# Layer with two head groups: x requested one column set ahead, its scaling and transposes paced anew, second token tile four steps behind, bonus matmuls three steps later

## The chip, the cores and the metric

The kernel runs on one core of a Trainium2 chip. The metric is device time in microseconds (us) of one execution, the median of several. Engines are named as in the profile: PE is TensorE (matmuls and transposes), ACT is ScalarE, DVE is VectorE, POOL is GpSimd, SP is SyncE, which here issues nearly all DMAs, in order, in one queue.

## The reference, cut to what matters

One layer on x of 4096 tokens by 1024 (float32): a normalised input is projected by one matrix to 4224 columns, which feed two groups of heads.

```python
xn = rms_norm(h, norm_g[l], RMS_EPS)
proj = xn @ w_in[l]
...
rwkv_in = token_shift(proj[..., off_b:off_b + SHIFT_WIDTH], shift_mu[l])
r, k_b, v_b, wd, ad = jnp.split(rwkv_in, b_idx, axis=-1)
...
y = rwkv7_recurrence(r_h, hd_b(decay), k_h, v_h, kk, hd_b(a))
...
bonus = jnp.sum(r_h * k_h * r_k[l].astype(f32), axis=-1, keepdims=True) * v_h
o_b = (y + bonus.reshape(bsz, seq, W_RWKV)).astype(x.dtype) * jax.nn.silu(g_b)
...
mix = jnp.concatenate([o_a, o_b], axis=-1)
h = h + mix @ w_out[l]
return rms_norm(h, final_g, RMS_EPS)
```

Group A is softmax attention (left out above), group B the recurrence.

## The kernel before, in words

Three phases follow one another: phase 1 (projection, and beside it the recurrence), phase 2 (attention), phase 3 (output projection). The change touches phase 1 alone.

**Projection.** The tokens are cut into eight blocks of 512. For a block the scaled x lies transposed in SBUF as `xh` (rounded) and `xl` (the remainder), eight slices of 128 by 512 each; there is one such pair, overwritten block after block, in two halves of 256 tokens. A block has an r set (columns of group B) and an a set (group A). The sets are worked off in the order r0 a0 r1 a1 r2 a2 r3 r4 r5 r6 r7 a7 a6 a5 a4 a3. Each set is a row of jobs. Token jobs (`tm_part`, kinds VB, GB, V, GA; one stands first and one last in every set) make four token tiles of 128 by 512; feature jobs (`fm_groups`) make one or two feature tiles. A step is one call of `mm3`, three matmuls (L248, L249, L250): L248 and L249 read `xh`, L250 reads `xl`. A token job has two parts of 16 steps; in each part the second tile runs two steps behind the first. Steps of a token job are counted 0 to 31 below, and those of the job after it go on from 32. Weight tiles `w` come through a ring of eight: `release` frees one and issues the load of the one eight further on (L233). Results stand in three PSUM buffers `pjt`/`pjf`; those of GB and GA are read by ACT (L310) and then DVE (L311), after which the buffer is free.

**New tokens.** Where the block changes (11 times), the last job of a set brings the first half of the next block: `x_load` (two DMAs into the two buffers `xv`, L153), `x_norm` (two squares on ACT into PSUM buffers `jk`, L162; an addition on DVE; two POOL operations; a scaling on ACT, L166), then `x_trans`: four groups of four PE transposes into a PSUM buffer `pt` (L176), each followed by two copies on ACT (`xh`, L179) and two remainders on DVE (`xl`, L180). In the second part of that job the four groups stand after steps 17, 20, 23 and 26, and `x_load` of the second half at step 27. The first token job of the next set carries the second half: scaling after step 4 (36), transposes after steps 6, 8, 10 and 12 (38, 40, 42, 44).

**Recurrence.** Four generators share PE with the projection. After each step `tick` lets every one that isn't waiting run on; a generator that gave a negative number runs only at every fourth tick. `p1_unit` prepares 256 tokens (16 units, two halves each); its last part is the bonus: POOL multiplies (L506), eight small PE matmuls take the product (`pbn`, L524), ACT copies it out. Key a8 of the table W is the number of ticks from the stage before to these matmuls. `p2_unit` inverts small triangles on DVE (31 times L578 and L579), `c_stream` walks the 64-token chunks (PE L687, DVE L690, PE L695 and L702, DVE L712, PE L716 and L721, DVE L725 and L728), `o_stream` finishes group B. They use three PSUM buffers `pg` in turn, `jk` and `pt` too. PE's order is as the program writes it; on the other engines a scheduler sets the order when the program is built.

Of the kernel before, what the change touches and what calls it, by code (L numbers as in the profile page):

```python
# [25 lines left out]
W = dict(  # L26
    G=4,    xn=2, xl=1024, sw=1024, np=2, le=3, l0=8, gb=5, pj=3, sb=4, wb=8, tb1=7, wm=0,
    xw=2048, cw=512, pl=1, pelat=330, tb=3, pb=3, lag2=2.0, ms=40, a0=2, a1=2, a2=2, a3=2,
    a4=2, a5=2, a6=2, a7=2, a8=2, a9=2, b0=2, b1=2, b2=2, b3=2, b4=2, b5=2,
    b6=2, b7=2, b8=1, b9=1, c0=10, c1=8, c2=2, c3=2, c4=1, c5=1, c6=2, c7=3,  # L30
    c8=2, o0=2, o1=4, o2=2, o3=4, o4=2, o5=2, o6=1, held=5, el=1, pz=18, ld=14,
    ba=2,  df=[2, 2, 2, 2],
# [76 lines left out]
def _phase1(ctx, tc, nc, e):  # L109
# [38 lines left out]
    def x_load(b, t):  # L148
        xs = []
        for s in range(2):  # L150
            r0 = b * BT + t * 256 + s * 128
            xv = xp.tile([128, D], F32, tag="xv", name="xv", bufs=2)
            nc.sync.dma_start(xv, x[r0:r0 + 128, :])  # L153
            xs.append(xv)
        xraw[b, t] = xs
# [105 lines left out]
                yield  # L261
            evacs[p](po)

    def tm_part(n0, s0, evac, last, side_x):
        po = {}
        order = []
        for n in range(KD + 2):
            if n < KD:
                order.append((s0, n))
            if n >= 2:  # L270
                order.append((s0 + 1, n - 2))
        for s, k in order:
            if k == 0:
                po[s] = ps_j.tile([128, BT], F32, tag="pj", name="pjt")
            w = wt[n0 + k]
            sl = slice(128 * s, 128 * s + 128)
            mm3(po[s], xh[:, k, sl], xl[:, k, sl], w[:, 0].rearrange("p a c -> p (a c)"), w[:, 1].rearrange("p a c -> p (a c)"), k)
            if k == KD - 1:
                evac(s)(po[s])
            if last and s == s0 + 1:  # L280
                release(n0 + k)
            next(side_x, None)
            yield
# [33 lines left out]
    def paced(g, steps):  # L317
        for n in range(64):
            if n in steps:
                next(g, None)  # L320
            yield

    def x_half1(b):
        x_norm(b, 1)
        yield
        yield from x_trans(b, 1)
        if b == 0:
            xfree[0] = True
            raw_next()
# [6 lines left out]
    def x_norm0(b):  # L336
        x_norm(b, 0)
        yield

    def tile_job(i, kind, parts, evs, nxt):  # L340
        n0 = first_tile[i]
        if kind == "f":
            assert not bg
            yield from fm_groups(n0, parts, [ev(0) for ev in evs])
            return
        half1 = bg.pop(1, None)
        assert half1 is None or nxt is None
        if nxt is not None:
            x_load(nxt, 0)
        if half1 is not None:  # L350
            side = paced(x_half1(half1), (4, 6, 8, 10, 12, 13))
        else:
            side = paced(x_norm0(nxt) if nxt is not None else iter(()), (10,))
        yield from tm_part(n0, 0, evs[0], False, side)
        for _ in side:
            pass
        side = paced(x_half0(nxt) if nxt is not None else iter(()), (1, 4, 7, 10, 11))
        yield from tm_part(n0, 2, evs[0], True, side)
        for _ in side:
            pass  # L360
        if nxt is not None:
            bg[1] = nxt
# [34 lines left out]
    def main():  # L397
        x_norm(0, 0)
        yield from x_trans(0, 0)
        x_load(0, 1)  # L400
        bg[1] = 0
        for _ in range(RING):
            prep()
        for i, (k, parts, evs, nxt, rdone) in enumerate(jobs):
            yield from tile_job(i, k, parts, evs, nxt)
            if rdone:
                done_r[0] += 1
# [1044 lines left out]
```

## Time and profile before

| | us |
|---|---|
| median of 3 runs | 3769.85 (3767.56 to 3772.0) |
| the profiled execution | 3761.58 |
| its span, first to last instruction | 3759.9 |
| busy in the span: PE, DVE, ACT, POOL | 3609.4, 2632.4, 1922.4, 761.2 |

The profile names a group of instructions by source line, engine, operation and tiles (written<-read). An instruction's idle time is that of its engine just before it, with what ended it. The granted clock is TensorE's, as a share of full speed (2.4 GHz). Phase 1 ends at 2135 us of the span, phase 2 at about 3380.

### The profile page before, as it was taken

The page shows a single profiled execution, that of the slowest core. Times are in us where ns is not written, and L with a number is a line of the kernel's source. Part 1 is how long each engine was busy: PE and PEld are TensorE (multiplying, and loading weights), DVE is VectorE, ACT ScalarE, POOL GpSimd, SP SyncE. Part 2 cuts the span into 40 slices and gives each one's busy share as a digit, 9 for nine tenths or more (in the row PEclk, how much of TensorE's full clock was granted, in tenths as well). Part 3 has the DMA queues.
Part 4 walks back from the last instruction along what each step waited for, and adds up shares of the span by engine and source line. Part 5 has one row for each costly group of instructions (what it writes and reads, how often), then busy time and mean ns, then how long its engine had stood idle before and what let it go on. Part 6 is the DMA issues. An engine that isn't in the chain of part 4 may idle for free.

```text
span 3759.9 us, 69957 instructions
## 1 busy us (share of the span) xinstructions
PE 3609.4 (96%) x26370; PEld 3050.9 (81%) x26370; DVE 2632.4 (70%) x5882; ACT 1922.4 (51%) x4042; POOL 761.2 (20%) x1156
## 2 busy tenths in 40 slices
PE   7999999999999999998999999999999999989999
PEld 5777777777777778777777789999999999978887
DVE  3566666667767787757777588898898898863333
ACT  4452352444445443444444377787787787761111
POOL 0112211211212222212221032222222222211000
PEclk9999999999999999999999999999999999999999
DMA  7976665666555565665675651141141131033332
GB/s 231 354 267 204 209 212 198 222 204 225 192 192 190 191 226 174 215 209 196 221 239 200 204 122 48 41 113 37 49 104 49 38 82 40 21 134 121 134 134 74
DMA packets 346092, 593.60 MB, mean 158 GB/s; under 512 B 55193, under 2 KB 210329, under 8 KB 345754
## 3 DMA queue, kind: packets, MB, share of 16 engines
q1 hardware_dynamic: 344602, 587.62, 48.4%
q8 instruction: 208, 3.41, 0.4%
q10 hardware_dynamic: 1152, 1.51, 0.1%
q14 instruction: 130, 1.06, 0.1%
HBM read 434.85 MB, written 154.14 MB: 157 GB/s over the span
## 4 chain that ended last, share of the span: by engine, by line
PE 75%; DVE 13%; DMA 4%; ACT 3%; issue 2%; SPq 2%; POOL 1%; DVEq 0%; POOLq 0%; ACTq 0%
PE po L1222 12%; PE ps L1127 6%; PE ps L1126 6%; PE tp L1197 6%; PE pjf L248 5%; PE pjf L250 4%; PE pjf L249 4%; PE pjt L248 4%; PE pjt L250 4%; PE pjt L249 4%; PE po L1372 3%; PE po L1371 3%; PE po L1370 3%; DVE DG L578 2%; DVE TL L579 2%
## 5 line engine op out<-in xcount | busy, mean ns | idle before, releaser
L1159 ACT ACTIVATE ring<-ring,nm 128x2048 f32<-128x2048 f32 (+14 forms) x472 | 589.0, 1253 | 31.3 <-DVE nm L1151 30.2
L1141 DVE CUSTOM_DVE_ANT_0 ring<-ps,zcol 128x1024 f32<-128x1024 f32 (+6 forms) x464 | 485.2, 1058 | 109.2 <-PE ps L1127 103.1
L1222 PE MATMUL po<-v,pt 128*128 128x128 f32 x4224 | 539.5, 276 | 10.0 <-ACT pt L1210 5.4
L1222 PEld LDWEIGHTS po<-v,pt 128*128 128x128 f32 x4224 | 517.9, 192 | 28.5 <-ACT pt L1210 7.3
L1126 PE MATMUL ps<-k,ta 128*128 128x512 f32 (+3 forms) x1152 | 483.1, 420 | 7.3 <-DMA ta<-q_d 4.9
L248 PE MATMUL pjt<-w,xh 128*128 128x512 f32 x1024 | 436.2, 426 | 29.1 <-DMA w<-ws_d 13.4
L248 PE MATMUL pjf<-xh,w 128*128 128x512 f32 x1088 | 451.1, 415 | 6.0 <-ACT w L236 4.5
L1127 PE MATMUL ps<-k,tb 128*128 128x512 f32 (+3 forms) x1152 | 432.0, 379 | 0.0
L250 PE MATMUL pjf<-xh,w 128*128 128x512 f32 x1088 | 431.0, 396 | 0.5 <-DVE w L237 0.5
L249 PE MATMUL pjf<-xl,w 128*128 128x512 f32 x1088 | 429.9, 395 | 0.0
L249 PE MATMUL pjt<-w,xh 128*128 128x512 f32 x1024 | 410.5, 401 | 0.9 <-DVE w L237 0.9
L250 PE MATMUL pjt<-w,xl 128*128 128x512 f32 x1024 | 410.0, 401 | 0.1
L1182 DVE SCALAR_TENSOR_TENSOR ring<-ring,rho 128x512 f32<-128x512 f32 (+3 forms) x600 | 407.1, 702 | 1.6
L1210 ACT COPY pt<-tp 128x512 f32<-128x512 f32 (+3 forms) x576 | 303.1, 550 | 194.0 <-PE tp L1197 188.7
L1197 PE MATMUL tp<-ident,ring 128*128 128x128 f32 x2112 | 313.6, 274 | 3.7 <-DVE ring L1182 3.7
L1197 PEld LDWEIGHTS tp<-ident,ring 128*128 128x128 f32 x2112 | 254.6, 142 | 40.6 <-issue 3.7
L248 PEld LDWEIGHTS pjt<-w,xh 128*128 128x128 f32 x1024 | 199.0, 194 | 80.9 <-DMA w<-ws_d 20.3
L248 PEld LDWEIGHTS pjf<-xh,w 128*128 128x128 f32 x1088 | 207.3, 191 | 57.4 <-ACT w L236 6.5
L250 PEld LDWEIGHTS pjf<-xh,w 128*128 128x128 f32 x1088 | 207.0, 190 | 49.2 <-DVE w L237 2.7
L1126 PEld LDWEIGHTS ps<-k,ta 128*128 128x128 f32 x1152 | 219.2, 190 | 32.8 <-issue 5.0
L1127 PEld LDWEIGHTS ps<-k,tb 128*128 128x128 f32 x1152 | 220.1, 191 | 23.4
L249 PEld LDWEIGHTS pjf<-xl,w 128*128 128x128 f32 x1088 | 208.0, 191 | 38.1
(205 smaller groups left out, 6421.4 us busy)
## 6 DMA issues: line engine op xcount, KB each, us to landing
w<-ws_d SPq DMA_DIRECT2D x448, 512.0 KB, 5.3
ws_d<-w SPq DMA_DIRECT2D x64, 512.0 KB, 5.3
xv<-in_x_dram SPq DMA_DIRECT2D x48, 512.0 KB, 5.4
ta<-q_d SPq DMA_DIRECT2D x128, 128.0 KB, 2.9
tb<-q_d SPq DMA_DIRECT2D x128, 128.0 KB, 3.0
k<-k_d SPq DMA_DIRECT2D x32, 512.0 KB, 7.1
mi<-mix_d SPq DMA_DIRECT2D x32, 512.0 KB, 3.3
xi<-in_x_dram SPq DMA_DIRECT2D x32, 512.0 KB, 4.2
```

Source lines behind the costliest of these rows:

```text
L248: nc.tensor.matmul(po, ah, bh, start=(k == 0), stop=False)
L249: nc.tensor.matmul(po, ah, bl, start=False, stop=False)
L250: nc.tensor.matmul(po, al, bh, start=False, stop=(k == KD - 1))
L1126: nc.tensor.matmul(ps[:, c:c + w], rr(ta[:, m, qs]), rr(k[:, m, c:c + w]), start=True, stop=False)
L1127: nc.tensor.matmul(ps[:, c:c + w], rr(tb[:, m, qs]), rr(k[:, m, c:c + w]), start=False, stop=True)
L1141: nc.vector.tensor_tensor_reduce(rg(m, ro, x), st["ps", b, m][:, c - 1024 * b:c - 1024 * b + x], msk, 0.125, -3.0e38, ALU.add, ALU.max, ac ...
L1159: nc.scalar.activation(rg(m, ro, x), rg(m, ro, x), AF.Exp, bias=st["nm"][:, m:m + 1], accum_out=st["lp"][:, m, j:j + 1])
L1182: nc.vector.scalar_tensor_tensor(rg(0, ro, x), in0=rg(1, ro, x), scalar=st["rho"], in1=rg(0, ro, x), op0=ALU.mult, op1=ALU.add)
L1197: nc.tensor.transpose(tp[:, j], rg(0, c, 128), ident)
L1210: nc.scalar.copy(pt[:, :n], st.pop(("tp", g))[:, :n])
L1222: nc.tensor.matmul(st["po"], pt[:, j], vt[h, kb // 8][:, kb % 8], start=(kb == 0), stop=(kb == i))
L1370: nc.tensor.matmul(po, mh[:, k], wh[k][:, fs], start=(k == 0), stop=False)
```

## The change

The first half of x is asked for one job earlier (before the job ahead of the last one), unless the last job's weights come fresh from the input, which is so at the first of the 11 changes of block; its scaling then stands at step 3 in place of 10, and its transposes after steps 16, 19, 21 and 24, with `x_load` of the second half at step 25. For that second half (not in block 0) the scaling moves to step 5 of the next token job (37) and the transposes to steps 12, 14, 17 and 20 (44, 46, 49, 52): two groups now stand inside its second part. In the second part of every token job the second tile runs four steps behind the first, so weight tiles 0 to 4 of such a job are released at steps 21, 23, 25, 27, 28 in place of 19, 21, 23, 25, 27. a8 goes from 2 to 5.

```diff
-    a4=2, a5=2, a6=2, a7=2, a8=2, a9=2, b0=2, b1=2, b2=2, b3=2, b4=2, b5=2,
+    a4=2, a5=2, a6=2, a7=2, a8=5, a9=2, b0=2, b1=2, b2=2, b3=2, b4=2, b5=2,
...
-    def tm_part(n0, s0, evac, last, side_x):
+    def tm_part(n0, s0, evac, last, side_x, lag):
         po = {}
         order = []
-        for n in range(KD + 2):
+        for n in range(KD + lag):
             if n < KD:
                 order.append((s0, n))
-            if n >= 2:
-                order.append((s0 + 1, n - 2))
+            if n >= lag:
+                order.append((s0 + 1, n - lag))
...
+        if half1 is not None:
+            side = paced(x_half1(half1), (5, 12, 14, 17, 20, 21) if half1 else (4, 6, 8, 10, 12, 13))
+        elif nxt is not None:
+            if (nxt, 0) not in xraw:
+                x_load(nxt, 0)
+                side = paced(x_norm0(nxt), (10,))
+            else:
+                side = paced(x_norm0(nxt), (3,))
+        else:
+            side = iter(())
+        yield from tm_part(n0, 0, evs[0], False, side, 2)
         if nxt is not None:
-            x_load(nxt, 0)
-        if half1 is not None:
-            side = paced(x_half1(half1), (4, 6, 8, 10, 12, 13))
-        else:
-            side = paced(x_norm0(nxt) if nxt is not None else iter(()), (10,))
-        yield from tm_part(n0, 0, evs[0], False, side)
-        for _ in side:
-            pass
-        side = paced(x_half0(nxt) if nxt is not None else iter(()), (1, 4, 7, 10, 11))
-        yield from tm_part(n0, 2, evs[0], True, side)
+            for _ in side:
+                pass
+            side = paced(x_half0(nxt), (0, 3, 5, 8, 9))
+        yield from tm_part(n0, 2, evs[0], True, side, 4)
...
         for i, (k, parts, evs, nxt, rdone) in enumerate(jobs):
+            if i + 1 < len(jobs) and jobs[i + 1][3] is not None and not tiles[min(first_tile[i + 1], len(tiles) - 1)][3]:
+                x_load(jobs[i + 1][3], 0)
             yield from tile_job(i, k, parts, evs, nxt)
```

The request for x on SP's queue, at the change from block 1 to block 2. First the order before: the two `xv` loads that end the excerpt's middle are the first half of block 2.

```order
L314 DMA ga_d<-st 128x512
L314 DMA vb_d<-st 128x512
L153 DMA xv<-in_x_dram 128x1024 x2
L314 DMA vb_d<-st 128x512
L233 DMA w<-ws_d 128x1024 x8
```

And in the changed kernel:

```order
L314 DMA ga_d<-st 128x512
L314 DMA vb_d<-st 128x512 x2
L153 DMA xv<-in_x_dram 128x1024 x2
L233 DMA w<-ws_d 128x1024 x3
L314 DMA vb_d<-st 128x512
```

In both these loads stand in the first job of the set, right behind the second half of block 1, some 100 rows ahead of the job that scales them; one store of `vb_d` has moved ahead of them.

PE around the third group of transposes of a second half, at the change from block 4 to block 5; `xv_10069` and `xv_10071` (`xv_10020` and `xv_10022` in the changed kernel) are its tokens, and the numbers of `w` tell the weight tile, so the slice. Before:

```order
L176 MATMUL pt_10229<-ident_71,xv_10071 128x128
L248 MATMUL pjt_10150<-w_10067,xh_123 128x512
L249 MATMUL pjt_10150<-w_10067,xh_123 128x512
L250 MATMUL pjt_10150<-w_10067,xl_124 128x512
L248 MATMUL pjt_10132<-w_10125,xh_123 128x512
L249 MATMUL pjt_10132<-w_10125,xh_123 128x512
L250 MATMUL pjt_10132<-w_10125,xl_124 128x512
L176 MATMUL pt_10251<-ident_71,xv_10069 128x128
```

And now:

```order
L176 MATMUL pt_10245<-ident_71,xv_10022 128x128
L248 MATMUL pjt_10238<-w_10018,xh_123 128x512
L249 MATMUL pjt_10238<-w_10018,xh_123 128x512
L250 MATMUL pjt_10238<-w_10018,xl_124 128x512
L248 MATMUL pjt_10238<-w_10040,xh_123 128x512
L249 MATMUL pjt_10238<-w_10040,xh_123 128x512
L250 MATMUL pjt_10238<-w_10040,xl_124 128x512
L248 MATMUL pjt_10238<-w_10051,xh_123 128x512
L249 MATMUL pjt_10238<-w_10051,xh_123 128x512
L250 MATMUL pjt_10238<-w_10051,xl_124 128x512
L176 MATMUL pt_10273<-ident_71,xv_10020 128x128
```

Before, the steps behind the group work on the first half's tokens. Now they are those of tile `pjt_10238`, which is made of the second half: its third step (`w_10051`, slice 4) reads what this group has just transposed, two steps behind it.

The end of phase 1 on DVE, from the last but one `svu<-svu,WC` to the first instruction of phase 2. Before:

```order
L728 TENSOR_TENSOR svu<-svu,WC 64x256 x2
L690 COPY xs<-pc 128x256
L712 TENSOR_TENSOR svu<-pc,RN 64x256 x2
L725 TENSOR_TENSOR svu<-pc,svu 64x256 x2
L728 TENSOR_TENSOR svu<-svu,WC 64x256 x2
L757 TENSOR_REDUCE nm<-yv 128x8
L311 SCALAR_TENSOR_TENSOR st<-st,pjt 128x512
L758 SCALAR_TENSOR_TENSOR yv<-nm,yv 128x512
L1141 ISA ring,mx<-ps,mz 128x128
```

And now (each line of the source stands seven further down):

```order
L735 TENSOR_TENSOR svu<-svu,WC 64x256 x2
L311 SCALAR_TENSOR_TENSOR st<-st,pjt 128x512
L697 COPY xs<-pc 128x256
L719 TENSOR_TENSOR svu<-pc,RN 64x256
L311 SCALAR_TENSOR_TENSOR st<-st,pjt 128x512
L719 TENSOR_TENSOR svu<-pc,RN 64x256
L732 TENSOR_TENSOR svu<-pc,svu 64x256 x2
L735 TENSOR_TENSOR svu<-svu,WC 64x256 x2
L764 TENSOR_REDUCE nm<-yv 128x8
L1148 ISA ring,mx<-ps,mz 128x128
```

The last chunk of the recurrence now stands behind both last readings of `pjt`; on PE its last two groups, which stood 12 and 4 steps ahead of the projection's end, stand behind its last matmul. All along phase 1 the triangles and the chunks stand 8 steps later against the projection than before, the bonus matmuls of a unit's two halves 12 and 16 (4 and 8, then 12 and 16, up to block 3).

## Rows read from the trace of the kernel before

**Rows 1.** Windows: busy us (and count) per engine, granted clock, DMA share, GB/s.

```profile
140.00:2135.00 1995.00, 1906.75 (x15504) 1542.46 (x15504) 1369.15 (x3037) 843.08 (x1894) 418.31 (x415) 0.98 0.64 212
```

**Rows 2.** Waits of PE, 140 to 2135 us: total us, times, longest.

```profile
PE pt L176 <- ACT xv L166: 19.8, 15, 4.1
PE pjt L248 <- DMA w<-ws_d: 13.4, 12, 2.9
PE pbn L524 <- POOL rr L506: 13.3, 3, 5.2
PE pt L176 <- DVE xl L180: 11.9, 5, 4.5
PE pjt L248 <- DVE st L311: 11.7, 7, 4.0
```

**Rows 3.** Windows around two stalls.

```profile
1044.00:1058.00 14.00, 10.30 (x48) 8.42 (x48) 9.41 (x16) 9.98 (x22) 4.49 (x5) 0.88 0.31 85
1282.00:1298.00 16.00, 13.03 (x96) 10.46 (x96) 10.56 (x18) 9.62 (x23) 3.50 (x3) 0.68 0.68 219
```

**Rows 4.** Timeline of PE (start, us, then the instruction) behind another stall.

```profile
1176.40 0.63 PE L249 MATMUL pjt<-w,xh 128*128 128x512 f32 x1
1176.83 0.63 PE L250 MATMUL pjt<-w,xl 128*128 128x512 f32 x1
...
1181.02 0.40 PE L249 MATMUL pjt<-w,xh 128*128 128x512 f32 x1
1181.25 0.40 PE L250 MATMUL pjt<-w,xl 128*128 128x512 f32 x1
```

**Rows 5.** Timeline, a second half: its loads on SP, its first transposes on PE.

```profile
1032.73 1.05 SPq L153 DMA_DIRECT2D xv<-in_x_dram  x2
...
1046.98 0.33 PE L176 MATMUL pt<-ident,xv 128*128 128x128 f32 x1 [4.13 <-ACT xv L166]
```

**Rows 6.** Timeline, the next first half: its loads on SP, its first square on ACT.

```profile
1205.82 1.06 SPq L153 DMA_DIRECT2D xv<-in_x_dram  x2
...
1304.31 0.60 ACT L162 ACTIVATE jk<-xv 128x512 f32<-128x512 f32 x1
```

**Rows 7.** Timeline of ACT and PE in the last job of set r5.

```profile
1158.42 0.60 ACT L162 ACTIVATE jk<-xv 128x512 f32<-128x512 f32 x1 [6.48 <-DVE RN L479]
...
1170.14 0.50 PE L248 MATMUL pjt<-w,xh 128*128 128x512 f32 x1 [3.73 <-DVE st L311]
```

**Rows 8.** Timeline of POOL, DVE and PE at a bonus.

```profile
1282.72 1.80 POOL L506 TENSOR_TENSOR rr<-rr,f 128x512 f32<-128x512 f32 x1 [12.77 <-DVE WC L509]
...
1282.72 2.35 DVE L513 TENSOR_TENSOR BKF<-f,lw 64x512 f32<-64x512 f32 x2
...
1284.58 1.87 PE L524 MATMUL pbn<-rks,rr 128*128 128x2 f32 x8 [4.75 <-POOL rr L506]
```

**Rows 9.** Timeline, transposes and the first remainder behind them: a loaded and a quiet case.

```profile
258.59 0.60 PE L176 MATMUL pt<-ident,xv 128*128 128x128 f32 x4
...
263.70 0.88 DVE L180 SCALAR_TENSOR_TENSOR xl<-pt,g_t,xh 128x256 fp32r<-128x256 f32 x2
...
910.39 0.60 PE L176 MATMUL pt<-ident,xv 128*128 128x128 f32 x4
...
911.53 0.48 DVE L180 SCALAR_TENSOR_TENSOR xl<-pt,g_t,xh 128x256 fp32r<-128x256 f32 x1 [1.01 <-ACT xh L179]
```

**Rows 10.** Timeline, the end of phase 1 on DVE, PE and SP.

```profile
2127.88 0.86 DVE L712 TENSOR_TENSOR svu<-pc,RN 64x256 f32<-64x256 f32 x2 [3.13 <-PE pc L695]
...
2131.02 0.69 PE L716 MATMUL pc<-svu,bkt 128*64 128x64 f32 x16
...
2132.66 0.87 DVE L728 TENSOR_TENSOR svu<-svu,WC 64x256 f32<-64x256 f32 x2
...
2133.68 0.38 SPq L1025 DMA_DIRECT2D v<-v_d  x1
...
2140.38 0.73 PE L1126 MATMUL ps<-k,ta 128*128 128x512 f32 x1 [4.87 <-DMA ta<-q_d]
```

## The prediction

> **What bounds the kernel now.** I read first the page's sum: PE is busy 3609.4 of 3759.9 us, so TensorE is the bound and other engines matter only where it waits for them. The change touches phase 1 alone, so I next took that stretch after the start-up [rows 1]: PE busy 1906.75 of 1995 us, hence 88 us idle, at a mean granted clock of 0.98. Third came the list of PE's waits there [rows 2]. Five rows bear on the edits: new tokens not yet scaled (19.8), weights (13.4), the bonus product (13.3), copies that still hold a `pt` buffer (11.9), and L311 holding a `pjt` buffer (11.7). Together that is 70 us; no other wait is aimed at.
>
> Last I looked at what an idle stretch costs afterwards. Around a 4.13 us stall the clock is 0.88 over 14 us, and around a 4.75 us stall 0.68 over 16 us [rows 3]. Behind another stall matmuls follow at a pitch of 0.43 us, and a little later at 0.23 [rows 4]: PE ran at the 1.2 GHz level and then at 2.4 again, having idled before the fall. At the low level, 0.20 of each 0.43 us is lost (0.465). The mean of 0.98 over 1995 us means 4% of the stretch, about 80 us, at the low level, which loses 37 us. I spread these over the 88 us idle: every us of idle costs some 0.42 us more, so I multiply idle time by **1.42**. This is an average: some short gaps cost nothing, and the stall at 1284 cost about 16 x 0.32 x 2 x 0.465 = 4.8 us besides its own 4.75 [rows 3, 8].
>
> **The change part by part.** The sum is made against the profiled execution, 3761.58 us; the median is 8.3 us above it, so I add that at the end. A change under 0.2% (7.5 us) can hardly be told from none.
>
> *Early request of the first half: nothing.* The order shows these loads standing a set ahead already, and so does the trace: issued at 1205.82, first read at 1304.31 [rows 6], 98 us later. If that cover were gone, a load needs some 14 us from issue to first transpose, as in rows 5, and step 0 to step 17 of the old job would just have covered it.
>
> *Earlier scaling of the first half: nothing by itself.* ACT's squares get seven more steps. In set r5 they waited 6.48 us for a shared buffer with ACT's queue behind them, and PE then stalled 3.73 us for L311 [rows 7]; such an event is counted under L311 below.
>
> *Pacing of the second half: -27.7.* From its loads at 1032.73 to its first transposes at 1046.98 are 14.25 us, of which PE waited 4.13 [rows 5]. One step takes about 1.0 us: phase 1 has 32 token tiles x 8.25 column jobs x 8 slices = 2112 steps in 2135 us. Before, the loads stood at step 27 and the first transposes at step 38, 11 us for a need of 14. Now they stand at 25 and 44, 19 us. The cover holds with 5 us to spare, and the row of 19.8 us [rows 2] should go but for about 0.3: -19.5 x 1.42 = -27.7.
>
> *What that pacing makes tight: +14.* The third group makes slices 4 and 5; the first tile of the second part reads slice 4 two steps behind it (the third step of that tile in the order), and the fourth group's slice 6 as closely. Two steps are about 2 us; in the clear they are worth 2 x 0.69 + 0.46 = 1.84 us, three matmuls a step at 0.23. Between them must lie the ACT copies and the DVE remainders. In a quiet case the remainder starts 1.0 us after its transposes end and ends 0.5 later (910.39 + 0.60, 911.53 + 0.48); in a loaded one the pair ends at 264.58 (263.70 + 0.88), 5.4 us after the transposes (258.59 + 0.60) [rows 9]. The quiet one fits, the loaded one is 3.5 us late, and a second late group adds about 1.5. There are eleven changes of block. I take two as loaded, 2 x 5 us x 1.42 = +14, nearer the quiet row because DVE works 1369 of 1995 us [rows 1] and ACT and DVE mostly had the groups done in time before. Ends: 0, and +78 if all eleven are loaded.
>
> *Second tile four steps behind: -11.4.* A token job's third and fourth tiles need a `pjt` buffer each, and L311 must have left it. The fourth now asks about 2 us later. Of 11.7 us in 7 waits, the longest 4.0 [rows 2] and the other 3.73 [rows 7] keep about 1.9 each; the small ones, 4 us together, go: -8 x 1.42. Ends: 0 (the delay only moves ACT's queue) and -16.6 (all).
>
> *The same lag for the weights: +6.* Tiles 0 to 4 are released one or two steps later in each of 32 token jobs; the next job's loads leave later and its slack falls from 11 steps to 9. SP's queue is in order, so each such load also holds back the stores and x loads behind it. PE waited 13.4 us in 12 such places [rows 2]; I take 4 us more, at 1.42. Ends: 0, and +18 if twelve places lose 1 us or more (two steps of 0.69 us bare is the most one can lose: 12 x 1.38 = 16.6, and one new place).
>
> *Bonus matmuls three ticks later: -16.* PE waited 13.3 us in three places [rows 2]; at 1284.58 it waited 4.75 for L506, which POOL could start only at 1282.72 and which took 1.80 [rows 8]. The matmuls stand about four steps later against their own unit, so waits of 4.75, 5.2 and 3.4 leave about 2 us: -11.3 x 1.42. Ends: -18.9, and 0 if the delay is eaten (first rival). Rows 8 show POOL's L506 and DVE's L513 starting in the same instant, 1282.72, and both running on. The Trainium skill (SBUF — State Buffer, "Who interferes with whom") has it otherwise: VectorE with two SBUF inputs and GpSimd share ports under a lock held for a whole instruction, and the issue order says who is blocked. By that rule L506 would wait out each L513, and this term would be near 0 and the sum near -19. This trace shows no such exclusion at that place.
>
> *Buffers `pt`: -3.5.* Of 11.9 us [rows 2] the second half's groups, now two and three steps apart, lose some 2.5; the first half's last groups are as far apart as before or closer. Ends: -17 (all go), +11 (the closer groups of all first halves wait 0.7 us more).
>
> *The end of phase 1: +4.* The recurrence stands 8 steps later, so its last two PE groups come behind the last projection matmul (2135). After that: DVE's two L712 (0.86) with an L311 between them now, about 1.7 us in all with the links; then from PE's L716 to the end of L728 2.5 us (2131.02 to 2133.53); SP's load of `v` follows L728 (2133.68), `ta` is queued behind it, and PE restarts at 2140.38, 6.85 us after L728 [rows 10]. So 11 us instead of 5.4 from the last matmul to the restart, less the 2 us of PE work moved out of the projection and its own links: +3.5 to +5. No factor, since there is one such place.
>
> *What the scheduler redraws elsewhere:* 0, ends -10 and +10; the recurrence meets other steps of the projection than before, and no row tells which.
>
> Sum: -27.7 + 14 - 11.4 + 6 - 16 - 3.5 + 4 = **-34.6**, so 3727 for the profiled execution and **3735** for the median.
>
> **The rivals.** *The bonus wait comes back (18%).* The triangles and chunks move 8 steps and the bonus more, so L506 may meet the same DVE load at another place. For it: POOL waited 12.77 us for DVE at 1282.72 [rows 8], more than the four steps gained. Against it: only three of 32 halves waited at all. Then the term of -16 is lost: 3751. The Trainium skill's lock, above, would give the same by another way, and rows 8 speak against it.
>
> *Slower: the wait moves from the transposes to the matmuls behind them (12%).* Without the +14 the sum is -48.6. Eleven second halves eat it up at 4.4 us each; at the loaded row's 5 us idle each, 7.1 with the clock, they cost 78, and the time is 3769.85 - 48.6 + 78 = 3799. For it: two steps of cover against a chain through two engines and two queues, which the old pacing did not ask for, having all groups done before the second part began. Against it: the quiet row needs only 1.5 us.
>
> *Everything fits (8%).* No late remainder, no weights lost, all `pt` and bonus waits gone: -34.6 - 14 - 6 - 13.4 - 3 = -71, so 3699.
>
> *The changes only swap waits (7%).* The pacing does what the early request would have done, and that request moves nothing [rows 6]; if ACT and DVE are late by as much in the new places as x was in the old, 3770.
>
> **How the numbers follow.** My forecast has 55%, the rivals 18, 12, 8 and 7. Predicted is the forecast's 3735. Its own range, from the ends of the tight pacing, the weights and the redrawn waits, is 3710 to 3760. The whole range takes in the bonus rival and the swapped waits above, and the nearer half of the large gain below: 3703 to 3770, leaving out the slower case and half of the best one. Faster by over 0.2%: the forecast nearly whole (52), most of the bonus rival (14) and the large gain (8), 74%. Within 0.2%: the swap and the edges of the first two, 13%. Slower: its rival and a little of the swap, 13%.
>
> **What would show it.** Right: after 140 us PE's wait of `pt` for `xv` is nearly gone, that of `pbn` is under 4 us in all, that of L311 under 5, the mean clock of the stretch is 0.99, and the gap at the end of phase 1 has grown to 8 or 9 us. A new row, `pjt` waiting for `xl` or `xh`, should hold about 10 us; at 50 the slower rival is true. The weights' row should grow by some 4. If `xv` waits remain, the load is later than its issue suggests and the first term falls; if idle time falls by 30 us but the clock stays at 0.98, the factor of 1.42 is wrong.

## The result, and the profile after

The changed kernel takes 3803.11 us (four runs, 3796.49 to 3803.45) against 3768.70 for the kernel before: a ratio of 1.0086, interval 1.0068 to 1.0103. It is slower by 34 us in these medians, and by 32 in the ratio, which is used below; 35 us less were forecast. Line numbers from 410 on stand seven higher in its profile.

Phase 1 now ends at 2171.9 us instead of 2135.0. Its busy time, columns as in [rows 1]:

```profile
140.00:2172.00 2032.00, 1916.16 (x15513) 1547.56 (x15511) 1369.35 (x3037) 840.98 (x1897) 419.21 (x415) 0.97 0.62 209
```

PE was idle 115.8 us in place of 88. PE's waits there, as in [rows 2]:

```profile
PE pjt L248 <- DMA w<-ws_d: 30.4, 28, 3.6
PE pjt L248 <- DVE st L311: 11.0, 3, 5.5
PE pa L465 <- DVE xl L180: 9.5, 4, 3.5
PE pjt L250 <- DVE xl L180: 8.9, 8, 2.0
PE pc L723 <- DVE svu L719: 8.4, 6, 3.1
PE pt L176 <- DVE xl L180: 7.3, 3, 4.1
PE ptt L620 <- ACT Zs L606: 5.8, 3, 3.5
PE pjt L248 <- DVE sl L301: 5.4, 1, 5.4
PE pjt L248 <- DVE carry L292: 4.3, 2, 2.3
...
PE pjt L248 <- ACT xh L179: 3.1, 2, 2.2
```

The aimed waits did go: `xv`, 19.8 us before, is down to 2.5, `pbn` from 13.3 to nothing. But weights have doubled, L311 has not moved, and seven rows are new or larger. To place the loss, phase 1 is cut in both kernels at the same step (924, four steps before set r3 ends). First the kernel before, then the changed one:

```profile
140.00:895.00 755.00, 726.72 (x5492) 588.00 (x5492) 500.17 (x1108) 311.64 (x695) 145.18 (x145) 0.98 0.66 224
895.00:2135.00 1240.00, 1180.03 (x10014) 954.46 (x10013) 868.99 (x1930) 531.44 (x1199) 273.13 (x270) 0.97 0.63 205
```

```profile
140.00:927.00 787.00, 736.90 (x5499) 592.75 (x5498) 494.47 (x1107) 307.70 (x691) 145.15 (x145) 0.98 0.64 216
927.00:2172.00 1245.00, 1179.25 (x10015) 954.81 (x10013) 874.88 (x1931) 533.28 (x1206) 274.06 (x270) 0.97 0.61 205
```

32 of the 37 us are lost in the first part, 22 of them as idle time (755 - 726.7 = 28.3 before, 787 - 736.9 = 50.1 now). There the sets alternate between r and a, up to step 792.

The end of phase 1, timeline of PE and SP, answers to [rows 10]:

```profile
2167.47 0.39 PE L250 MATMUL pjt<-w,xl 128*128 128x512 f32 x1
...
2170.05 0.69 PE L723 MATMUL pc<-svu,bkt 128*64 128x64 f32 x16 [1.28 <-DVE svu L719]
...
2172.70 0.38 SPq L1032 DMA_DIRECT2D v<-v_d  x1
...
2178.45 0.76 PE L1133 MATMUL ps<-k,ta 128*128 128x512 f32 x1 [5.95 <-DMA ta<-q_d]
```

From the end of the last projection matmul (2167.86) to the restart are 10.6 us.

### The profile page after: what moved, and what is told of

It reads as the page before. It is cut to its first block, busy times and chain, and to the rows that moved or that the text cites. A ratio compares the mean times of both kernels' runs of the same rounds, so it can differ in the third digit from the quotient of the medians.

```text
span 3801.1 us, 69959 instructions
## 1 busy us (share of the span) xinstructions
PE 3618.4 (95%) x26370; PEld 3055.8 (80%) x26370; DVE 2632.0 (69%) x5882; ACT 1919.1 (50%) x4042; POOL 763.0 (20%) x1156
## 3 DMA queue, kind: packets, MB, share of 16 engines
q10 hardware_dynamic: 1152, 1.51, 0.1%
## 4 chain that ended last, share of the span: by engine, by line
PE 70%; DVE 13%; DMA 4%; ACT 3%; issue 2%; POOL 1%; SPq 0%; DVEq 0%; POOLq 0%; ACTq 0%
PE po L1229 12%; PE ps L1134 6%; PE ps L1133 6%; PE tp L1204 6%; PE pjf L248 4%; PE pjf L250 4%; PE pjf L249 4%; PE pjt L248 4%; PE pjt L250 3%; PE pjt L249 3%; PE po L1379 3%; PE po L1378 3%; PE po L1377 3%; DMA w<-ws_d 2%; DVE TL L586 2%
## 5 line engine op out<-in xcount | busy, mean ns | idle before, releaser
L248 PE MATMUL pjt<-w,xh 128*128 128x512 f32 x1024 | 441.0, 431 | 61.1 <-DMA w<-ws_d 30.4
L250 PE MATMUL pjf<-xh,w 128*128 128x512 f32 x1088 | 430.6, 396 | 0.6 <-DVE w L237 0.6
L250 PE MATMUL pjt<-w,xl 128*128 128x512 f32 x1024 | 415.2, 406 | 9.0 <-DVE xl L180 8.9
L249 PE MATMUL pjt<-w,xh 128*128 128x512 f32 x1024 | 415.6, 406 | 1.1 <-DVE w L237 1.1
L250 PEld LDWEIGHTS pjt<-w,xl 128*128 128x128 f32 x1024 | 200.4, 196 | 60.5 <-DVE xl L180 15.1
L250 PEld LDWEIGHTS pjf<-xh,w 128*128 128x128 f32 x1088 | 207.0, 190 | 49.1 <-DVE w L237 2.7
```

The costliest lines, as they stand in the source:

```text
L248: nc.tensor.matmul(po, ah, bh, start=(k == 0), stop=False)
L249: nc.tensor.matmul(po, ah, bl, start=False, stop=False)
L250: nc.tensor.matmul(po, al, bh, start=False, stop=(k == KD - 1))
```

## The experiments

Times below are the ratio to the kernel before and its interval, with the difference as a share of 3770 us. Repeats of one kernel spread by 0.3 to 0.5%, and a wait comes from one profiled execution, so a wait that differs by two or three us is not read. The parts: **lag** (fourth tile four steps behind), **pacing** (second half), **early** (request, with the first half scaled after step 3 and its groups at steps 16 to 24), **bonus** (a8=5).

### Each part undone

```diff
# lag undone
-        yield from tm_part(n0, 2, evs[0], True, side, 4)
+        yield from tm_part(n0, 2, evs[0], True, side, 2)
# pacing undone
-            side = paced(x_half1(half1), (5, 12, 14, 17, 20, 21) if half1 else (4, 6, 8, 10, 12, 13))
+            side = paced(x_half1(half1), (4, 6, 8, 10, 12, 13))
# early undone: the request ahead of the job is taken out, and
-            side = paced(x_half0(nxt), (0, 3, 5, 8, 9))
+            side = paced(x_half0(nxt), (1, 4, 7, 10, 11))
# bonus undone
-    a4=2, a5=2, a6=2, a7=2, a8=5, a9=2, b0=2, b1=2, b2=2, b3=2, b4=2, b5=2,
+    a4=2, a5=2, a6=2, a7=2, a8=2, a9=2, b0=2, b1=2, b2=2, b3=2, b4=2, b5=2,
```

Lag undone:

> The changed kernel with the second tile of the second part two steps behind the first again (as before); all else as changed. Theory weights (the later release of weight tiles 0 to 4 makes PE wait for weights: 30.4 us in 28 places in the changed kernel, 13.4 in 12 before): the wait falls by about 17 us, the time by 17 x 1.3 = 22, to 3781. Theory pacing (the second half's groups are too close to their users): the lag of four gave the two last groups nothing, time stays near 3803 or rises by up to 5, and the weights' wait stays near 30. Theory recurrence (three ticks more shift the recurrence against the projection): stays within 5 of 3803.

Pacing undone:

> The changed kernel with the second half's scaling and transposes back after steps 4, 6, 8, 10 and 12; all else as changed. Theory pacing: waits of pjt and pa on xl and xh (21.5 us in the changed kernel) go, waits of pt on xv come back only in part because the load is two steps earlier (10 of the former 19.8 us): 11 us x 1.4 less, 3788; at the price of the slower rival, 3740. Theory weights: xv waits of 10 to 20 us come back and as much on xl goes, so 3795 to 3810, with the weights' wait still near 30. Theory recurrence: the same, near 3803.

Early undone:

> The changed kernel without the early request, with the first half's scaling and transposes paced as before; all else as changed. The prediction said that the request does nothing: 3803 within 5. Theory queue (a first half requested a job early stands ahead of weight loads in SP's queue and makes PE wait for weights): the weights' wait falls from 30.4 towards 13 and the time by up to 22, to 3781.

Bonus undone:

> The changed kernel with the bonus matmuls two ticks after their stage again. Theory recurrence (three ticks more shift the whole recurrence by 8 steps, so its DVE work meets the copies of the projection in other places: new waits of ptt on Zs, of pjt on carry and sl, some 17 us): these go, the bonus waits of 13 come back: 3795 to 3803. Theory weights or pacing alone: the bonus waits of some 13 us come back and nothing else moves: 3815 to 3822.

Measured: lag undone 1.0028 (1.0018 to 1.0039), pacing undone 0.9995 (0.9985 to 1.0005), early undone 1.0042 (1.0027 to 1.0056), bonus undone 0.9990 (0.9981 to 0.9999). So undoing any one part gives back 17 to 36 us, 109 together, of a loss of 32: the parts clash, and none is the only cause. Lag undone met its forecast for the weights, but not all that went was weights. PE's waits in that run:

```profile
PE pjt L248 <- DVE st L311: 28.6, 12, 5.8
PE pjt L248 <- DMA w<-ws_d: 11.2, 15, 2.8
```

The lag takes 17.6 us from L311 and gives 19 to the weights. The theories for pacing and for bonus were too small (forecast 3788 to 3810 and 3795 to 3822, measured 3768 and 3766), and the queue theory of early fell: weights stayed at 28. With pacing undone the weights stay as well (32.5 us), while what waits on `xl` and `xh` falls from 28.8 to 12.6 and all idle time from 115.8 to 104.5, some 16 us with the clock. Why pacing undone gives back 34 us stays open.

### Parts alone

The same edits made on the kernel before; "pacing and early" is the changed kernel with lag and bonus undone.

> The kernel before with the lag of four steps alone. The prediction's terms: 11.4 us less for the pjt buffers and 6 more for the weights, so 3766. Theory trade (what the fourth tile no longer waits for L311, the next job waits for its weights; seen in the changed kernel against the one with the lag undone, where 17.6 us less on L311 stand against 20.4 more on weights): L311 falls from 11.7 to about 2, the weights rise from 15 to about 30, so 5 us of idle more, and 3776 to 3782.

> The kernel before with the new pacing of the second half alone. The prediction's terms: 27.7 less, 14 more, 3.5 less: 3754. Slower rival: 50 us of new waits on xl and xh, so near 3800. Theory swap (xv goes, waits of pjt and pa on xl and xh take its place, some 20 us): 3765 to 3775.

> The kernel before with the bonus matmuls three ticks later alone. The prediction's terms: 16 us less for the bonus product, 4 more for the end of phase 1, so 3760. Theory recurrence (its whole order against the projection moves 8 steps; in every run with five ticks the waits of ptt on Zs, of pjt on carry, sl and others stand some 25 us above the kernel before): pbn goes from 13.3 to 0 and those rise by 20 to 25, so 10 us of idle more, and with the clock and the end of phase 1 3785 to 3792.

> The changed kernel with lag and bonus both undone: new pacing and early request, nothing else. The prediction's terms: 3754. Theory trade and theory recurrence together (both undone parts cost): below the 3770 of the kernel with the bonus alone undone by about 5 to 8, so 3762 to 3765, with the weights' wait near 13 and L311 near 10.

Measured in this order: lag 1.0007 (0.9997 to 1.0017), pacing **0.9977** (0.9966 to 0.9987), bonus 1.0038 (1.0025 to 1.0050), pacing and early 1.0006 (0.9997 to 1.0014). Pacing alone is a gain of 9 us. Bonus alone costs 14, close to what theory recurrence gave. Its waits:

```profile
PE pt L176 <- ACT xv L166: 26.7, 19, 5.2
PE pjt L248 <- DVE st L311: 19.0, 10, 5.0
...
PE ptt L618 <- ACT Zs L604: 5.9, 2, 3.7
PE pjt L248 <- DVE sl L301: 5.6, 1, 5.6
```

No `pbn` row is left, as forecast, but x and L311, which the edit does not touch, wait 7 us more each. Early costs 11 us on top of pacing, where nothing was forecast. In lag alone L311 falls from 11.7 to 3.3 us and the weights rise from 15.0 to 22.7: theory trade has the direction right, but the two nearly cancel, and the time stays.

### Pairs, the shift alone, the request alone, other places for the groups

```diff
# shift alone, on the kernel before
-        yield W["b3"]
+        yield W["b3"] + (8 if u in (0, 2, 4, 6) else 0)
# pacing and request, first half as before (lag and bonus undone too)
-                side = paced(x_norm0(nxt), (3,))
+                side = paced(x_norm0(nxt), (10,))
-            side = paced(x_half0(nxt), (0, 3, 5, 8, 9))
+            side = paced(x_half0(nxt), (1, 4, 7, 10, 11))
# groups between old and new places, alone and in the changed kernel
-            side = paced(x_half1(half1), (5, 12, 14, 17, 20, 21) if half1 else (4, 6, 8, 10, 12, 13))
+            side = paced(x_half1(half1), (5, 9, 11, 13, 15, 16) if half1 else (4, 6, 8, 10, 12, 13))
```

Pacing and bonus:

> New pacing of the second half and the bonus three ticks later, without lag and early request. Alone the first gave -9 us, the second +14. Theory sum (the parts add): +5, so 3774. Theory meeting (undoing either one in the changed kernel gave 33 us, more than both cost alone, because the recurrence, 8 steps later, puts its pa matmuls and its DVE work beside the later groups): pa on xl stands at 5 us or more, pt on xl and use of xl at 20, and the time is +15 to +25: 3784 to 3794.

The shift alone:

> The kernel before with the inverse of four units started eight ticks later: triangles, chunks and later units stand where the changed kernel has them, while a unit's bonus keeps its two ticks. Theory recurrence (the move of eight steps is what the bonus edit cost): inverse, carry, sl and other waits rise by about 20 us, and if the bonus waits of 13 us stay the time is 3770 + 14 + 18 = 3800; at least 3782. Theory bonus (the later bonus matmuls themselves do it): the time stays within 5 us of 3770.

Pacing and request:

> New pacing of the second half and the early request, but the first half scaled after step 10 and transposed after steps 17, 20, 23 and 26 as before. With its own pacing the early request cost 13.6 us over the pacing alone. Theory queue (the loads stand elsewhere in SP's queue, and weights wait 7 us more): 3768 to 3775, weights near 24. Theory first half (scaling seven steps earlier and tighter groups make it): 3757 to 3762, weights near 17.

The groups between, alone:

> The kernel before with the second half scaled after step 5 and transposed after steps 9, 11, 13 and 15 of the next token job (41, 43, 45, 47), between the old and the new places; all else as before. Theory swap (the new places cost 10.8 us at the matmuls that use xl, and the old ones 19.8 at the transposes; between them both fit): xv under 4 us, use of xl under 2, so 10.8 x 1.4 = 15 below the new pacing alone, 3744 to 3750. Theory displacement (DVE is late by as much wherever the groups stand): waits of pt on xl rise instead, 3757 to 3765.

Lag and pacing:

> New pacing and lag, without bonus and early request. Theory meeting (the lag costs 22 us only where the recurrence stands 8 steps later: +20 behind pacing, early request and bonus, but +1 on the kernel before and -3 to -6 with pacing and early request): 3752 to 3760, weights behind an x load under 6 us. Theory pacing with lag (the lag takes two steps from the room of the third and fourth group): use of xl rises from 10.8 to 20 and the time to 3775 or more.

The groups between, in the changed kernel:

> The changed kernel with the second half's groups after steps 9, 11, 13 and 15 (41 to 47) instead of 12 to 20. Theory tightness (groups two and three steps ahead of their users are the cost of the pacing in the changed kernel, 33 us over the old places): waits of use and of pa on xl and xh fall from 21.5 to under 5 and the time by 16 x 1.4 to some 3780. Theory displacement (DVE is late by as much wherever the groups stand): pt on xl rises by as much, and the time stays at 3795 to 3805.

Measured: pacing and bonus 0.9983 (0.9973 to 0.9993), shift alone 1.0010 (1.0000 to 1.0021), pacing and request 0.9978 (0.9967 to 0.9988), groups between alone 0.9978 (0.9968 to 0.9988), lag and pacing 0.9977 (0.9966 to 0.9988), groups between in the changed kernel 1.0069 (1.0057 to 1.0081). What follows:

- The request costs nothing. The first half's earlier scaling and tighter groups cost about 11 us (1.0006 against 0.9978).
- The shift of inverse and chunks costs 4 us, not the 12 to 30 of theory recurrence. The rest of the bonus edit's 14 us must then lie in what this run leaves in place: the bonus matmuls themselves, and `pw` and `pa` of a unit, which the bonus edit moves by up to 12 steps in the first part of phase 1. Which of them it is, no run shows.
- Two parts by themselves don't lose: pacing with bonus (theory meeting gave 3784 to 3794, measured 3764), or with lag, is a gain.
- Tightness as the pacing's price falls. With the groups earlier, waits of the projection on `xl` go, but the recurrence's take their place. On the kernel before, too, theory displacement holds: with the groups between, `pt` waits 22.7 us for `xl`, with the new pacing 9.9. Waits of the changed kernel with the groups between:

```profile
PE pa L465 <- DVE xl L180: 14.3, 5, 4.9
...
PE pgg L558 <- DVE xl L180: 3.9, 2, 2.0
PE pjt L250 <- DVE xl L180: 2.8, 3, 2.0
```

`pa` and `pgg` read no x. They take one of the three `pg` buffers in turn, which `pt` holds until the copies to `xl` are done. The timeline of PE in the changed kernel:

```profile
509.22 0.60 PE L176 MATMUL pt<-ident,xv 128*128 128x128 f32 x4
509.57 0.36 PE L465 MATMUL pw<-wah,lrh 128*128 128x256 f32 x1
509.77 0.28 PE L466 MATMUL pw<-wah,lrl 128*128 128x256 f32 x1
512.49 0.55 PE L465 MATMUL pa<-wah,lrh 128*128 128x256 f32 x1 [2.44 <-DVE xl L180]
```

### Why the lag costs 22 us with bonus and nothing without

First the position of the loads in the program. On the changed kernel, the order of tiles of the lag of two, releases at the steps of the lag of four:

```diff
-            if last and s == s0 + 1:
-                release(n0 + k)
+            if last and p in (5, 7, 9, 11, 12, 13, 14, 15):
+                release(n0 + (5, 7, 9, 11, 12, 13, 14, 15).index(p))
```

> The changed kernel with the second tile two steps behind again, but the weight tiles released at the later steps of the lag of four (21, 23, 25, 27, 28). Against the kernel with the lag undone (3784, weights 11.3, L311 28.6) only the releases are later. Theory release (the later release is what the lag cost): the weights' wait rises to near 30 and the time by 20 x 1.3 = 26, to 3810, since nothing is won back at L311. Theory order (the order of the tiles does it, by the room left to the second half's groups): weights under 15 and time within 5 of 3784.

Measured 1.0033 (1.0022 to 1.0044), weights 11.9 us. But the order of SP's queue is that of lag undone except for two stores, so no load was moved, and the run doesn't decide between the theories. On the chip the loads of `w` wait for PE's last readings (SP waited for L250 of `pjt` 134 times, 195.1 us), and those were not moved here.

Then the load of x behind all releases:

```diff
-            side = paced(x_half0(nxt), (0, 3, 5, 8, 9))
+            side = paced(x_half0(nxt), (0, 3, 5, 8, 15))
```

> The changed kernel with the load of the second half of x at step 31 of the last job in place of 25, behind all its weight releases. In the changed kernel 14.4 of 31.7 us of weight waits stand 5 to 14 us behind such a load, in the kernel before none. Theory queue (the load of x goes ahead of three weight loads and they come late): those 14 us go, xv waits rise by some 5 us as its cover shrinks from 19 to 13 steps: 10 us x 1.3 less, 3790. Theory release alone (two steps later is enough to be late): weights stay near 30 and with the xv waits the time is 3805 to 3810.

Measured 1.0071 (1.0057 to 1.0085). It decides nothing: the scheduler put the loads of x back behind the second weight load of the next set, where they stood, and SP's whole order is that of the changed kernel.

The trace shows what that place means. Timeline of SP at the change from block 1 to 2, kernel before, and the loads of weights issued ahead of x and behind it, with KB and us to landing:

```profile
497.36 0.32 SPq L233 DMA_DIRECT2D w<-ws_d  x1
...
499.51 3.19 SPq L233 DMA_DIRECT2D w<-ws_d  x3
503.40 0.81 SPq L153 DMA_DIRECT2D xv<-in_x_dram  x2
504.30 2.41 SPq L233 DMA_DIRECT2D w<-ws_d  x3
```

```profile
w<-ws_d SPq DMA_DIRECT2D x4, 512.0 KB, 3.8
...
w<-ws_d SPq DMA_DIRECT2D x3, 512.0 KB, 7.3
```

The same in the changed kernel:

```profile
516.36 2.15 SPq L233 DMA_DIRECT2D w<-ws_d  x2
520.15 0.81 SPq L153 DMA_DIRECT2D xv<-in_x_dram  x2
521.05 3.32 SPq L233 DMA_DIRECT2D w<-ws_d  x4
```

```profile
w<-ws_d SPq DMA_DIRECT2D x2, 512.0 KB, 3.6
...
w<-ws_d SPq DMA_DIRECT2D x6, 512.0 KB, 9.5
```

Before, four of the eight tiles went ahead of the 1 MB of x; now two do, since the lag has the tiles read two steps longer and the load of x stands at step 25 in place of 27 (with early undone, so at step 27, three do). Tile 2 then stops PE at the third step of the next job, on PE's timeline:

```profile
528.63 0.50 PE L248 MATMUL pjt<-w,xh 128*128 128x512 f32 x1 [2.28 <-DMA w<-ws_d]
```

In the changed kernel 14.4 us of such waits stand within 15 us behind a load of x, in the kernel before none.

So the bytes of x were taken away and the order left:

```diff
-            nc.sync.dma_start(xv, x[r0:r0 + 128, :])
+            if t and b:
+                nc.sync.dma_start(xv[:, 0:128], x[r0:r0 + 128, 0:128])
+            else:
+                nc.sync.dma_start(xv, x[r0:r0 + 128, :])
...
-                    nc.tensor.transpose(pt[:, kk, 128 * s:128 * s + 128], xs[s][:, 128 * k:128 * k + 128], ident)
+                    nc.tensor.transpose(pt[:, kk, 128 * s:128 * s + 128], xs[s][:, 0:128] if t and b else xs[s][:, 128 * k:128 * k + 128], ident)
```

> The changed kernel with the second halves of x (not block 0's) loaded as 128 of their 1024 columns, so an eighth of the bytes, and these columns used eight times over in the squares and transposes; the scaling of a half is shorter by seven eighths. So these halves of x are not the reference's. Program order on PE and SP as in the changed kernel. Theory queue (weight loads issued behind the load of x share the transfer engines with its 1 MB and land 8 us after issue where those ahead need 4): the 14.4 us of weight waits behind an x load fall under 4 and the time by 11 x 1.4 = 15, to 3788. Theory read (the last reading of tiles 2 to 4 comes two steps later, and that alone is too late): 10 us or more of them stay and the time is within 6 of 3803.

Measured 1.0032 (1.0020 to 1.0043): 20 us less than the changed kernel, and 3.9 us left of the 14.4. Theory queue holds. All idle time fell by 11.3 us, the weights by 11.2; the `xv` row kept its 2.5. The shorter scaling of these halves may have given a little of the 20.

Why is the lag harmless without bonus? The order has the same crossing there (in lag and pacing three tiles go ahead of x), but only 1.9 us of such waits; with the bonus undone, where two go ahead, they are 4.5 of 29.0 us. What PE does between the crossing and the use differs. Lines on PE in the kernel before, 504 to 511.5 us, from the load of x to past the change of set:

```profile
L248 PE MATMUL pjt<-w,xh 128*128 128x512 f32 x9 | 3.6, 404 | 0.0
...
L524 PE MATMUL pbn<-rks,rr 128*128 128x2 f32 x8 | 1.0, 241 | 0.0
L458 PE MATMUL pw<-wah,lrh 128*128 128x256 f32 x2 | 0.6, 283 | 0.0
L459 PE MATMUL pw<-wah,lrl 128*128 128x256 f32 x2 | 0.6, 282 | 0.0
L459 PE MATMUL pa<-wah,lrl 128*128 128x256 f32 x2 | 0.6, 282 | 0.0
L458 PE MATMUL pa<-wah,lrh 128*128 128x256 f32 x2 | 0.6, 281 | 0.0
```

And in the changed kernel, 521 to 528.7, all of its groups:

```profile
L248 PE MATMUL pjt<-w,xh 128*128 128x512 f32 x9 | 3.6, 401 | 2.3 <-DMA w<-ws_d 2.3
L250 PE MATMUL pjt<-w,xl 128*128 128x512 f32 x8 | 3.1, 390 | 0.0
L249 PE MATMUL pjt<-w,xh 128*128 128x512 f32 x8 | 3.1, 390 | 0.0
```

Before, sixteen matmuls of the recurrence filled PE while the weights came; now nothing stands there but the projection, and the wait takes their place. The changes of block stand at steps 264, 528, 792, 928, 1064, 1200, 1336, 1600, 1728, 1856 and 1984. Within five steps of them, the kernel before has 16, 16, 16, 128, 16, 132, 100, 24, 72, 96 and 100 recurrence matmuls, and so have lag and pacing, and the kernel with bonus undone. The changed kernel, and that with early undone, have none at 264, 528, 792, 928 and 1600, 8 at 1064 and 1728, and 100 to 140 at the other four. The 14.4 us stand behind the five changes with none, except 1.3 us behind 1728. By this reading the move of the recurrence took away, at these places, what had covered the loads. It is not the whole price of the lag: in all five pairs of runs it also adds 7 to 10 us at `xl` and `xh`, and without bonus it raises the weights too, by 5 to 8 us, against 18 to 20 with it. That bonus has this effect on the lag is shown by the runs (the lag costs 22 us on top of pacing and bonus, 0 on top of pacing alone, and on top of pacing and early 22 with bonus and -6 without); that the missing matmuls are how, I take from the traces, and no run put them back alone.

### What is left with the two losing parts undone

Bonus back at two ticks, first half scaled and transposed as before; lag, pacing and request stay.

```diff
-    a4=2, a5=2, a6=2, a7=2, a8=5, a9=2, b0=2, b1=2, b2=2, b3=2, b4=2, b5=2,
+    a4=2, a5=2, a6=2, a7=2, a8=2, a9=2, b0=2, b1=2, b2=2, b3=2, b4=2, b5=2,
-                side = paced(x_norm0(nxt), (3,))
+                side = paced(x_norm0(nxt), (10,))
-            side = paced(x_half0(nxt), (0, 3, 5, 8, 9))
+            side = paced(x_half0(nxt), (1, 4, 7, 10, 11))
```

> The changed kernel with the bonus back at two ticks and the first half scaled and transposed as before: lag, pacing of the second half and early request stay. Theory meeting (the two parts undone make the loss, and the lag is harmless without them): 3755 to 3762, the gain of pacing alone or a little more. Theory sum with the lag's cost kept (20 us as in the changed kernel): 3780.

Measured 0.9981 (0.9972 to 0.9989): 7 us faster than before. Faster than both kernels are this one, pacing alone, lag with pacing, pacing with bonus, the groups between alone, pacing with request, and by less the changed kernel with bonus undone. The intervals of the first six overlap, so a smallest edit, **the pacing of the second half alone** (0.9977), is the one to keep.

## Why the prediction was wrong

Idle time of PE in phase 1 after 140 us by what it waited for (us, summed from the waits of each trace; "rest" is recurrence, feature jobs and small ones), and the time at the low clock level:

| | before | changed | lag undone | bonus undone | early undone | pacing alone | bonus alone | small x |
|---|---|---|---|---|---|---|---|---|
| weights | 15.0 | 31.7 | 11.3 | 29.0 | 29.9 | 17.3 | 17.0 | 20.5 |
| L311 | 11.7 | 11.0 | 28.6 | 1.8 | 5.5 | 11.1 | 19.0 | 13.3 |
| xl, xh | 11.9 | 28.8 | 18.5 | 36.0 | 21.8 | 22.0 | 5.3 | 26.5 |
| xv | 19.8 | 2.5 | 2.5 | 1.0 | 8.9 | 1.5 | 26.8 | 2.5 |
| pbn | 13.3 | 0 | 0 | 7.2 | 0 | 10.4 | 0 | 0.8 |
| rest | 16.4 | 41.8 | 42.2 | 23.9 | 44.0 | 23.3 | 35.0 | 41.0 |
| sum | 88.0 | 115.8 | 103.0 | 98.8 | 110.1 | 85.5 | 103.2 | 104.5 |
| low clock | 92 | 123 | 109 | 99 | 116 | 89 | 120 | 130 |

By the steps of the prediction, in idle time before the factor:

- **Second half's cover, -19.5:** right, -17.3.
- **Bonus product, -11.3:** right by its row, -13.3. But the same edit brought more than it took. My reading of [rows 8], that L506 and L513 ran side by side without excluding each other, was wrong: a common start doesn't show that, the durations have to be compared. Shortest, median and longest (ns) of all of them in the kernel before, and the second L513 of [rows 8]:

```profile
L513 DVE TENSOR_TENSOR BKF<-f,lw x64: 673/1593/1785, 163.2 to 1971.3; 64x512 f32<-64x512 f32 x64
L506 POOL TENSOR_TENSOR rr<-rr,f x32: 1283/1487/1802, 163.3 to 1970.7; 128x512 f32<-128x512 f32 x32
1283.41 1.66 DVE L513 TENSOR_TENSOR BKF<-f,lw 64x512 f32<-64x512 f32 x1
```

  So at 1282.72 the second L513 ran 1.0 us over its shortest time, and L506, with 1.80, 0.5 over its own: they did hold each other up. That did not bring the term to 0, as I had tied to it: no `pbn` wait is left.
- **End of phase 1:** right; 11 us from the last matmul to the restart were forecast, 10.6 measured.
- **Early request, nothing:** right for the request. "Earlier scaling of the first half: nothing by itself" was wrong; that pacing costs 11 us without bonus and lag, 17 with both. Which of its two moves does it stays open.
- **Tight pacing, +10:** measured 21.5. The projection's own uses wait 12.0 (8.9 + 3.1), near the forecast, but in ten waits of at most 2.2 us and not in two of 5; the 9.5 of `pa` were not in the sum, because I had looked for users of x and not for users of the buffer.
- **Lag, -8 at L311:** the lag took 17.6 us (lag undone against changed), more than forecast; the bonus edit had first raised this wait (19.0 alone), so that the sum stayed.
- **Lag, +4 for the weights:** measured +16.7, at the upper end that I gave (16.6 us of idle time and one new place, which I took over as +18 of time without the factor of 1.42). I had counted steps of slack (11 to 9), not what stood in front of the load in the queue. At the change from block 1 to 2 tile 2 was issued behind x at 521.05 and PE's wait for it ended at 528.63, 7.6 us later, which nine bare steps of 0.69 (6.2) don't cover.
- **`pt` buffers, -2.5:** -4.6, right enough.
- **"What the scheduler redraws elsewhere: 0":** this is the step that failed most. The rest rose by 25 us, outside the bounds of 10 either way. Every run with a8 at 5 that the table shows has 35 to 44 there, every one with 2 has 16 to 24. I took a recurrence that moves with the bonus as neutral on average, and it was not. What rose are the recurrence's own waits for DVE and ACT (`pc` from 12.6 to 16.9, `ptt` from 1.1 to 9.4) and the projection's for `sl`, `carry` and `jk` (from nothing to 12.8). What held DVE and ACT up in each of them is not shown; the shift alone raises the rest to 29.7 and costs only 4 us.
- **Factor 1.42:** held. 31 us more at the low level times 0.465 are 14 us on 27.8 of idle, 1.51; by PE's busy time, which rose by 9.4 us (1906.75 to 1916.16), it is 1.34.

Forecast idle -27.3, measured +27.8: of the 55 us between them, 25 are the redrawn rest, 13 the weights, 11.5 the tight pacing, 7 L311, and 2 less from the others.

The slower rival gave 3799 and 3803 came, but that is chance, its mechanism is not what was measured: it wanted five us of idle time at each of eleven second halves from the projection's uses, which waited 12 us in all. The bonus rival (the wait comes back) is wrong as well: no `pbn` row is left.

## What to carry to other kernels

Interleaved work is also cover: before a stream is moved, look at what transfers land while it runs, at set and block changes above all, and count the steps left without it. An edit that is harmless alone can clash with another when it makes a load late and the other takes away what hid it, so measure them one by one and together. A wait for a buffer belongs to all users of its pool, and a load's slack is counted in its queue, behind the bytes ahead of it, not in steps. And whether two engines exclude each other is read from how long their instructions take together and apart, not from their starts.

## What the runs showed of the hardware

At the change from block 1 to 2, weight loads of 512 KB issued right behind the two loads of x (1 MB) landed after 7.3 us in the median (three loads, kernel before) and 9.5 (six, changed kernel), those ahead of them after 3.8 and 3.6. In the run with an eighth of x's bytes, the six loads behind it had a median of 7.2, so part of that is the weights queueing on each other.

More idle time cost clock: the time at the low level rose from 92 to 123 us as the idle time rose from 88 to 116. The proportion is not fixed: over the table it lies between 1.0 (bonus undone) and 1.24 us (small x) per us of idle time.

Of L506 on POOL and L513 on DVE in the kernel before, the one that started first took close to its shortest time. Where L506 was ahead by about 0.1 us, it took 1.31 to 1.37 us and L513 1.77 to 1.79; where L513 was ahead or started with it, L513 took 0.67 to 0.69 us and L506 up to 1.80.
